# The first stage of a two-layer trunk on one Trainium2 core: modulation made tile by tile, x loaded first, and a third a_u head in the stage

## The chip, the cores and the metric

The kernel runs on one core of one Trainium2 chip. TensorE multiplies matrices, VectorE (DVE) and ScalarE (ACT) do elementwise work, GpSimd (POOL) some small arithmetic, and SyncE (SP) issues all transfers from memory. The time is the device time of one execution in microseconds, given as the median of several runs. The matrices are in float32, kept exact by splitting each operand into a rounded part and a rest, so that one product becomes three matmuls.

## The reference

Two layers act on a latent stream x (256 tokens, 2048 features) and a context stream of the same size. Each layer first scales and shifts the normalised stream, with a scale and a shift that come from a vector c:

```python
shift, scale, gate = jnp.split(silu_c @ w_mod[l] + b_mod[l], 3, axis=-1)
shift_c, scale_c, gate_c = jnp.split(silu_cc @ w_mod[l] + b_mod[l], 3, axis=-1)
h = rmsnorm(x, g_pre[l]) * (1.0 + scale[:, None]) + shift[:, None]
h_c = rmsnorm(ctx, g_pre[l]) * (1.0 + scale_c) + shift_c
proj = h @ w_in[l]
proj_c = h_c @ w_in[l]
```

The 5120 columns of the projection feed three branches: a gated MLP with position mixing (columns a_u, a_v, a_g), windowed attention (q, k, v, b_g) and a Fourier mixing (c_x, c_g). In the first branch y_a = gelu(a_u) * mix(rmsnorm(gelu(a_v))) * silu(a_g), with four heads of 128 columns. The branches are joined, multiplied by w_out, normalised, gated and added to the stream. The output is the latent stream after the second layer.

## The kernel before

Features are cut into 16 k tiles of 128. The two streams stand side by side, features on partitions, as 16 tiles of 128 x 512: `yo[k]` holds x, and `hh[k]`, `hl[k]` hold the two parts of h. A weight of `w_in` is streamed in halves of a unit (128 x 1024, 512 KB): SP loads it to `raw` (three buffers), ScalarE casts it to `whi` (L367), VectorE takes the rest as `wlo` (L368; four buffers each). `W.next` hands out the next half and emits those that are to be made ahead; `NEAR` says how many at the start of a layer. TensorE's order is exactly that of the program. The other engines' orders are made by a planner, which goes by priority (program order, unless lowered) and lets an instruction whose buffer is not free be passed by another.

The modulation vector needs w_mod, whose shift and scale columns of layer 0 are 33.6 MB. `mod_start` makes them on TensorE in the first stage: for a group of four k tiles of c (`kg` 0 to 3) it loads a block of w_mod and issues four products with c as the 128 x 32 stationary operand, one for each quadrant of the bank `ps_mod` (L172). VectorE transposes the bank (L177), four small products sum the quadrants into `ps_modc` (L182), and VectorE makes `gs` and `sh`, the scale and shift of the tiles (L191 to L194). k tiles 0 to 7 go in four pairs (`PAIRS`, products 512 wide, loads of 256 KB into the buffers of the still unused tiles hh8 to hh15 and hl8 to hl15), k tiles 8 to 15 one by one (`ALONE`, products 256 wide, 512 KB loads or two of 256 KB). For the single tiles there are two sets of buffers, for even and for odd k.

`make_h` (L451, L455, L458) then turns x into h, and the loop over `blocks` in `layer` accumulates, k outermost, four banks of a_v (tokens on partitions, 12 matmuls a tile) and two banks of a_u (heads 0 and 1, six matmuls a tile), while the next block's modulation runs between. These six banks have the tag `mm`; the remaining two banks of PSUM have the tag `ms` and serve ps_mod, ps_modc and all small results. After the stage `branch_a` and `fourier_mats` are queued as later work, which is given back to TensorE in the middle of the following units when a count of product time (`later.tick`) has reached its due time. Then come units of 128 columns (`tunit`, 48 matmuls into `ps_t`): the heads 2 and 3 of a_u, c_x and so on. The rest of w_mod is multiplied on VectorE in steps that `pace` issues at a rate per unit.

At the start SP issues c, the vectors, the first constants, then x. ScalarE squares x tile by tile (L464, L467), VectorE adds the squares (L468), TensorE sums them over features (L427, L429), GpSimd takes the power (L414), VectorE and TensorE spread the result (L421, L433) and VectorE copies it as `rb0` (L1009). In TensorE's order this lies between the first groups of the first modulation block.

Of the kernel before, what the change touches and what calls it, by code (L numbers as in the profile page):

```python
# [13 lines left out]
P = 128  # L14
# [9 lines left out]
PAIRS, ALONE = [0, 2, 4, 6], list(range(8, KT))  # L24
# [3 lines left out]
def units():  # L28
    """(name, first column, columns, first k tile, k tiles): blocks of w_in of 128 x 2048 each."""
    u = []  # L30
    u += [("av", COL["av"], 512, 4 * i, 4) for i in range(4)]
    u += [("au01", COL["au"], 256, 8 * i, 8) for i in range(2)]
    u += [(f"au{h}", COL["au"] + 128 * h, 128, 0, 16) for h in (2, 3)]
    u += [(f"cx{h}", COL["cx"] + 128 * h, 128, 0, 16) for h in range(4)]
    u += [(f"ag{h}", COL["ag"] + 128 * h, 128, 0, 16) for h in range(4)]
    u += [(f"cg{h}", COL["cg"] + 128 * h, 128, 0, 16) for h in range(4)]
    u += [(f"k{h}", COL["k"] + 128 * h, 128, 0, 16) for h in range(2)]
    u += [("v", COL["v"], 256, 8 * i, 8) for i in range(2)]
    u += [(f"q{h}", COL["q"] + 128 * h, 128, 0, 16) for h in range(8)]
    u += [(f"bg{h}", COL["bg"] + 128 * h, 128, 0, 16) for h in range(8)]  # L40
    return u
# [25 lines left out]
def trunk_kernel(ctx: ExitStack, tc: tile.TileContext, xT, xhalf, cT, wss, wsl, wmod, win, wout0, wout1, const, vec, rows,  # L67
# [24 lines left out]
    # ---- constants  # L92
    ct = sb([P, KT, 2], F32, "ct")
    DMA.dma_start(ct, cT)
    vecs = sb([P, 2, NVEC], F32, "vecs")
    DMA.dma_start(vecs, vec)
# [13 lines left out]
    class low:  # L110
        """instructions that may wait for the next `n`."""
# [22 lines left out]
    # ---- modulation: columns [128, 16, stream] of scale, shift and gate  # L134
# [5 lines left out]
    def mod_cols(l, cb, ps8):  # L140
        """ps8 [128, 4, 2]: silu(c) @ w_mod for 512 columns of column block cb."""
        what, j0 = cb // 4, (cb % 4) * 4
        b = vc(l, "bmod")[:, cb * 4:cb * 4 + 4].unsqueeze(2).to_broadcast([P, 4, 2])
        sl = slice(j0, j0 + 4)
        if what == 0:
            V.tensor_tensor(out=sh[l][:, sl], in0=ps8, in1=b, op=ALU.add)
        else:
            dst = (gs[l] if what == 1 else gg0)[:, sl]
            g = vc(l, "gpre" if what == 1 else "gpost")[:, sl].unsqueeze(2).to_broadcast([P, 4, 2])
            V.scalar_tensor_tensor(out=dst, in0=ps8, scalar=1.0 if what == 1 else 0.0, in1=b,  # L150
                                   op0=ALU.add, op1=ALU.add)
            V.tensor_tensor(out=dst, in0=dst, in1=g, op=ALU.mult)

    def mod_start(k0, nk):
        """scale and shift of k tiles k0 .. k0 + nk - 1 of layer 0 on the tensor engine: yields after
        each unit's products, and before the columns."""
        ps = ms_ps("mod")
        n = 2 * P * nk
        for kg in range(4):
            src = wss[PAIRS.index(k0), kg] if nk == 2 else wsl[ALONE.index(k0), kg]  # L160
            if nk == 1:
                tags = (("mraw", "mraw", "macc", "vv"), ("mg", "mgl", "yo0 yo1", "yo2 yo3"))[k0 % 2][kg]
            else:
                tags = " ".join(f"{t}{8 + 2 * kg + i}" for i in range(2) for t in ("hh", "hl"))
# [31 lines left out]
    def mod_dve(l, cb, red):  # L196
        """red [128, 2, 16]: sums over the 32 partitions of each quadrant, transposed."""
# [38 lines left out]
    def mod_gate1():  # L236
        """products of silu(c) and the gate's columns of w_mod in layer 1, still to be summed over partitions."""
# [16 lines left out]
    def gate1():  # L254
        """(sum + b_mod) * g_post of layer 1's gate, on all partitions."""
# [23 lines left out]
    NEAR = [1] * 6 + [0] * 6 + [1, 2, 3]  # L279
# [7 lines left out]
    def pace():  # L287
        """steps of the modulation due per half of a unit, behind the latest weights on the vector engine."""
# [6 lines left out]
    # ---- work of other engines that hands products back to the tensor engine later  # L295
    class Later:
# [19 lines left out]
        def flush(self):  # L316
# [8 lines left out]
            (("yo8 yo9", 1), ("yo10 yo11", 1)), (("yo12 yo13", 1), ("yo14 yo15", 1))]  # L325
    BACK = 8

    # ---- weights: raw -> exact parts hi + lo, in halves of a unit, ahead of their use
    class Stream:
        AHEAD = 3  # L330

        def __init__(self):
            self.src, self.out, self.pos, self.stop = [], [], 0, 0
            self.place, self.behind = {}, {}
            for l in range(2):
                def half(name, i, h):
                    return win[l, UIDX[name][i], h]
                for i in range(2):
                    self.src += [half("av", 2 * i, 0), half("au01", i, 0), half("av", 2 * i, 1),
                                 half("av", 2 * i + 1, 0), half("au01", i, 1), half("av", 2 * i + 1, 1)]  # L340
                for i, u in enumerate(UNITS):
                    if u[0] not in ("av", "au01"):
# [45 lines left out]
    def part(w, c):  # L388
        """columns c of both parts; a part is a tile or a list of tiles side by side."""
# [19 lines left out]
    # ---- per-token reciprocal rms from sums over features  # L409
# [14 lines left out]
    def col_sums(ps, q, n, start=True, stop=True):  # L424
        """columns of ps: sums over the partitions of q [128, n * 128], one accumulation group."""
# [10 lines left out]
    # ---- streams in feature-major tiles  # L436
    yo = [None] * KT
# [7 lines left out]
    def make_h(l, k, rb, streams):  # L445
        """h = x * rstd * gs + sh, as hi + lo; rb: rstd over the tokens of `streams`."""
# [26 lines left out]
    def tunit(n, sl=None):  # L473
        """feature-major product of one unit of 128 columns: PSUM [128, n]."""
# [18 lines left out]
    blocks = [(k, 2) for k in PAIRS] + [(k, 1) for k in ALONE]  # L493

    # ---- one layer, up to the inputs of the output projection
    def layer(l):
# [12 lines left out]
        # a_v (token-major) and two heads of a_u, k outermost  # L509
        av = [mm_ps("av") for _ in range(nt)]  # L510
        au = [mm_ps("au") for _ in range(2)]
# [6 lines left out]
        def start_au(k):  # L518
            for j in range(2):
                c = slice((k % 4) * 256 + j * P, (k % 4) * 256 + (j + 1) * P)  # L520
                mm3(au[j][:, 0:n], part(auw, c), (hh[k][:, 0:n], hl[k][:, 0:n]), k == 0, k == KT - 1)
            later.tick(PASS * 512 * nt + PASS * n * 2)

        for i, (k0, nk) in enumerate(blocks):
# [13 lines left out]
            if k0 % 4 == 0:  # L538
                auw = W.next()
            for _ in range(2 if nk == 2 else 4):  # L540
# [38 lines left out]
        # branch A  # L579
        def branch_a():  # L580
            vt = [w2k([P, 512]) for _ in range(nt)]
            ss = sb([P, 4], F32, "ss")
            for j in range(2):
# [8 lines left out]
            yield 12.0 if l == 0 else 7.0  # L592
            for h in range(4):
# [9 lines left out]
                yield (12.0 if h == 1 else 2.0) if l == 0 else (7.0 if h == 1 else 2.0)  # L603

        # branch C
# [9 lines left out]
        def fourier(g, ps):  # L615
            """cos(2 pi t m / 256) is even in t around 128 and sin odd: positions t and 256 - t are added for the one
            and subtracted for the other, which leaves 128 rows each (position 128 in the sines' row of t = 0)."""
# [25 lines left out]
        # branch B  # L643
        def rope(hi, lo, ps):
            """x * cos + rot(x) * sin of the latents, and x of the context, as hi + lo."""
# [97 lines left out]
        for h in (2, 3):  # L743
# [56 lines left out]
    # ---- output projection  # L800
# [33 lines left out]
    def finish():  # L834
        """layer 1's output projection with tokens on partitions, and x1 + gate * y / rms(y)."""
        x1 = {}

        def turn():
            """x1 of the latents to tokens on partitions: [128, token tile, 512] per 512 columns."""
# [68 lines left out]
    def boundary(s, acc):  # L908
        """x1 = x0 + gate * y / rms(y) of stream s in place, and its own 1 / rms."""
# [79 lines left out]
    with tc.manual_schedule(engines={mybir.EngineType.PE}):  # L989
        # ---- start: modulation of the first k tiles, x and its statistics  # L990
        raw = w2k([P, NFIRST])
        DMA.dma_start(raw, const[:, 0:NFIRST])
        A.copy(identr, raw[:, 0:P])
        A.copy(cst[:, 0:NFIRST - P], raw[:, P:])
        for k in range(KT):
            yo[k] = sb([P, T], F32, f"yo{k}")
            DMA.dma_start(yo[k], xT[k])
        acc0 = sb([P, T], F32, "acc")
        for k in range(KT):
            add_sq(acc0, yo[k], FULL, k == 0)  # L1000
        m = mod_start(*blocks[0])
# [9 lines left out]
        W.emit()  # L1011
        W.emit()
# [82 lines left out]
```

## Time and profile before

| | us |
|---|---|
| time, median of 3 runs | 1171.78 (1170.43 to 1172.42) |
| span of the profiled execution | 1167.9 |
| TensorE busy in it | 1136.0 (97%) |
| VectorE busy | 881.8 (76%) |
| ScalarE busy | 509.8 (44%) |
| first a_v product starts | 37.37 |
| first product of the unit after the stage | 136.79 |

The median of the runs lies 3.9 us above the span of the profiled execution; no time of its own is given for that execution. In the lines of the profile, `ps_t<-hh,whi` means that the tile ps_t is written from hh and whi, `x48` is a count, and L172 is line 172 of the kernel. The chain of work that ended last is followed back from the last instruction, so a piece on it is work, or a wait counted into the piece before it, that the end hangs on. A busy share of 97% on TensorE is not a measure of its speed: products are pipelined, and their ends are modelled.

### The profile page before, as it was taken

To read this page: it belongs to the slowest core of one execution; us is meant where nothing else is said; L and a number is where in the kernel's file an instruction comes from. 1 tells how busy PE (TensorE), PEld (TensorE's weight loads), DVE (VectorE), ACT (ScalarE), POOL (GpSimd) and SP (SyncE) were. 2 spreads that over 40 slices of the span, in tenths; PEclk is the share of its full clock that TensorE was granted. 3 is DMA by queue.
4 is the path that set the end of the run, shared out by engine and by line. 5 is a ranking of instruction groups with operands and counts; after the bars stand their busy time and mean duration, and the time that the engine had idled before them with its cause. 6 is when DMAs were issued, how large, how long until landed. Compare 5 with 4: busy or idle time off the path is not lost.

```text
span 1167.9 us, 17483 instructions
## 1 busy us (share of the span) xinstructions
PE 1136.0 (97%) x6656; PEld 953.7 (82%) x6656; DVE 881.8 (76%) x1469; ACT 509.8 (44%) x914; POOL 17.3 (1%) x23
## 2 busy tenths in 40 slices
PE   3999999999999999999999999999999999999996
PEld 1466688888898888888888888889899999997885
DVE  5454498888988878798989886495896678888554
ACT  4222513322224667632533233365563278745442
POOL 0000000000000000000000000200000000000001
PEclk9999999999999999999999999999999999999998
DMA  9999765466665334455466665365656665688563
GB/s 339 378 387 357 254 196 166 145 202 193 200 200 178 105 114 136 134 175 173 158 199 209 205 216 162 109 207 173 205 158 205 203 200 178 195 269 244 190 187 120
DMA packets 73892, 234.32 MB, mean 201 GB/s; under 512 B 8528, under 2 KB 9680, under 8 KB 73808
## 3 DMA queue, kind: packets, MB, share of 16 engines
q1 hardware_dynamic: 73808, 233.21, 61.6%
q8 instruction: 52, 0.85, 0.3%
q14 instruction: 32, 0.26, 0.1%
HBM read 231.08 MB, written 2.10 MB: 200 GB/s over the span
## 4 chain that ended last, share of the span: by engine, by line
PE 92%; DVE 3%; DMA 2%; ACT 2%; issue 1%; POOL 0%; SPq 0%; DVEq 0%; ACTq 0%; POOLq 0%
PE ps_t L384 20%; PE ps_t L385 20%; PE ps_t L386 20%; PE ps_mod L172 3%; PE ps_av L384 2%; PE ps_y L386 2%; PE ps_y L384 2%; PE ps_y L385 2%; PE ps_av L385 2%; PE ps_av L386 2%; PE ps_v L386 1%; PE ps_v L384 1%; PE ps_v L385 1%; PE ps_tp L722 1%; PE ps_au L384 1%
## 5 line engine op out<-in xcount | busy, mean ns | idle before, releaser
L384 PE MATMUL ps_t<-hh,whi 128*128 128x512 f32 (+1 forms) x1296 | 452.1, 349 | 0.0
L386 PE MATMUL ps_t<-hh,wlo 128*128 128x512 f32 (+1 forms) x1296 | 447.4, 345 | 0.0
L385 PE MATMUL ps_t<-hl,whi 128*128 128x512 f32 (+1 forms) x1296 | 447.0, 345 | 0.0
L367 ACT CAST whi<-raw 128x1024 fp32r<-128x1024 f32 x218 | 228.2, 1050 | 397.3 <-PE ps_t L385 274.4
L368 DVE TENSOR_TENSOR wlo<-raw,whi 128x1024 fp32r<-128x1024 f32 x218 | 265.3, 1220 | 99.1 <-ACT whi L367 98.8
L384 PEld LDWEIGHTS ps_t<-hh,whi 128*128 128x128 f32 x1296 | 244.9, 189 | 34.3 <-issue 4.6
L386 PEld LDWEIGHTS ps_t<-hh,wlo 128*128 128x128 f32 x1296 | 244.7, 189 | 30.6
L385 PEld LDWEIGHTS ps_t<-hl,whi 128*128 128x128 f32 x1296 | 244.9, 189 | 28.9 <-issue 0.5
L209 DVE SCALAR_TENSOR_TENSOR macc<-mraw,cs,macc 128x512 f32<-128x512 f32 x360 | 249.9, 745 | 17.6 <-DMA mraw<-in_wmod_dram 17.5
L455 ACT ACTIVATE hh<-w2k,sh 128x256 fp32r<-128x256 f32 x64 | 29.0, 502 | 61.4 <-DVE w2k L451 61.4
L384 PE MATMUL ps_y<-whi,hh 128*128 128x512 f32 x112 | 45.0, 401 | 0.0
L386 PE MATMUL ps_y<-whi,hl 128*128 128x512 f32 x112 | 43.8, 392 | 0.0
L385 PE MATMUL ps_y<-wlo,hh 128*128 128x512 f32 x112 | 43.7, 390 | 0.0
L384 PE MATMUL ps_av<-whi,hh 128*128 128x512 f32 x96 | 40.0, 416 | 0.0
L385 PE MATMUL ps_av<-wlo,hh 128*128 128x512 f32 x96 | 37.9, 395 | 0.4 <-DVE wlo L368 0.4
L172 PE MATMUL ps_mod<-hh,kt 128*32 128x512 f32 x64 | 21.5, 649 | 17.0 <-DMA hh<-in_wss_dram 17.0
L386 PE MATMUL ps_av<-whi,hl 128*128 128x512 f32 x96 | 37.6, 392 | 0.0
L386 PE MATMUL ps_v<-whi,hl 128*128 128x256 f32 x128 | 36.2, 283 | 0.0
L384 PE MATMUL ps_v<-whi,hh 128*128 128x256 f32 x128 | 36.2, 283 | 0.0
L385 PE MATMUL ps_v<-wlo,hh 128*128 128x256 f32 x128 | 36.2, 283 | 0.0
L468 DVE TENSOR_TENSOR acc<-acc,w2k 128x512 f32<-128x512 f32 (+1 forms) x33 | 21.2, 641 | 18.7 <-ACT w2k L467 17.2
L401 ACT CAST w2k<-ps_tp 128x512 fp32r<-128x512 f32 x40 | 23.5, 587 | 22.8 <-PE ps_scc L385 12.0
(292 smaller groups left out, 1491.8 us busy)
## 6 DMA issues: line engine op xcount, KB each, us to landing
raw<-in_win_dram SPq DMA_DIRECT2D x160, 512.0 KB, 4.1
mraw<-in_wmod_dram SPq DMA_DIRECT2D x128, 512.0 KB, 4.3
raw<-in_wout_dram SPq DMA_DIRECT2D x64, 512.0 KB, 4.2
hh<-in_wss_dram SPq DMA_DIRECT2D x32, 256.0 KB, 5.6
hl<-in_wss_dram SPq DMA_DIRECT2D x32, 256.0 KB, 5.4
yo<-in_xT_dram SPq DMA_DIRECT2D x16, 256.0 KB, 5.4
mraw<-in_wsl_dram SPq DMA_DIRECT2D x8, 512.0 KB, 6.9
yo<-in_wsl_dram SPq DMA_DIRECT2D x16, 256.0 KB, 7.2
```

Of the source, the lines that this page charges most:

```text
L172: PE.matmul(ps[32 * kk:32 * kk + 32, 0:n], cpad[:, kg * 4 + kk], ws[kk], start=kg == 0, stop=kg == 3, tile_position=(0, 32 * kk))
L209: V.scalar_tensor_tensor(out=acc[:, s], in0=w[:, kk % 2], scalar=c, in1=acc[:, s], op0=ALU.mult, op1=ALU.add)
L367: A.copy(ph, r[:, c])
L368: self.last = V.tensor_tensor(out=pl, in0=r[:, c], in1=ph.bitcast(F32), op=ALU.subtract)
L384: PE.matmul(ps, st[0], mv[0], start=start, stop=False)
L385: PE.matmul(ps, st[0], mv[1], start=False, stop=False)
L386: PE.matmul(ps, st[1], mv[0], start=False, stop=stop)
L401: A.copy(hi, src)
L455: first = A.activation(hh[k][:, sl], t[:, sl], AF.Identity, bias=sh[l][:, k, s:s + 1])
L468: V.tensor_tensor(out=acc[:, sl], in0=acc[:, sl], in1=q[:, sl], op=ALU.add)
L722: PE.transpose(tp[:, (2 * j + b) * P:(2 * j + b + 1) * P], src, ident)
```

## The change

Layer 0's first stage is rewritten in three respects. All sixteen k tiles get their modulation one by one (`blocks` holds single tiles only), with other buffers for the odd tiles below 8. x is loaded first, with c behind its first tile, and the first constants and the vectors behind x; ScalarE's two copies of the constants come after the squares. And a third head of a_u (head 2) is accumulated in the stage, in one of the two `ms` banks, with its two weight halves in the buffers named in `AU2`; the unit au2 behind the stage goes, three halves are emitted before the stage instead of two, and the due times of `branch_a` in layer 0 are 9.0 and 4.0 instead of 12.0 and 12.0. Layer 1 keeps its two heads in the stage.

```diff
-PAIRS, ALONE = [0, 2, 4, 6], list(range(8, KT))
+PAIRS, ALONE = [0], list(range(KT))
...
-    ct = sb([P, KT, 2], F32, "ct")
-    DMA.dma_start(ct, cT)
+    yo = [sb([P, T], F32, f"yo{k}") for k in range(KT)]
+    for k in range(KT):
+        DMA.dma_start(yo[k], xT[k])
+        if k == 0:
+            ct = sb([P, KT, 2], F32, "ct")
+            DMA.dma_start(ct, cT)
     vecs = sb([P, 2, NVEC], F32, "vecs")
-    DMA.dma_start(vecs, vec)
...
-                tags = (("mraw", "mraw", "macc", "vv"), ("mg", "mgl", "yo0 yo1", "yo2 yo3"))[k0 % 2][kg]
+                odd = ("hh14 hl14", "hh15 hl15") if k0 < 8 else ("yo0 yo1", "yo2 yo3")
+                tags = (("mraw", "mraw", "macc", "vv"), ("mg", "mgl") + odd)[k0 % 2][kg]
...
-    NEAR = [1] * 6 + [0] * 6 + [1, 2, 3]
+    NEAR = [1] * 7 + [0] * 7 + [1, 2, 3]
...
+    AU2 = [(("hh12 hl12", 1), ("hh13 hl13", 1)), (("yo4 yo5", 1), ("yo6 yo7", 1))]
...
-                    self.src += [half("av", 2 * i, 0), half("au01", i, 0), half("av", 2 * i, 1),
+                    third = [half("au2", 0, i)] if l == 0 else []
+                    if l == 0:
+                        self.place[len(self.src) + 2] = AU2[i]
+                    self.src += [half("av", 2 * i, 0), half("au01", i, 0), *third, half("av", 2 * i, 1),
                                  half("av", 2 * i + 1, 0), half("au01", i, 1), half("av", 2 * i + 1, 1)]
...
-                    if u[0] not in ("av", "au01"):
+                    if u[0] not in ("av", "au01") + ("au2",) * (l == 0):
...
-    blocks = [(k, 2) for k in PAIRS] + [(k, 1) for k in ALONE]
+    blocks = [(k, 1) for k in ALONE]
...
-        au = [mm_ps("au") for _ in range(2)]
+        au = [mm_ps("au") for _ in range(2)] + [ms_ps("au") for _ in range(1 - l)]
...
+            if l == 0:
+                mm3(au[2], part(au2w, slice((k % 8) * P, (k % 8 + 1) * P)), (hh[k], hl[k]), k == 0, k == KT - 1)
...
+            if k0 % 8 == 0 and l == 0:
+                au2w = W.next()
...
-            for j in range(2):
+            for j in range(len(au)):
                 A.activation(ytmp(j), au[j][:, 0:n], AF.Gelu_apprx_tanh)
...
-            yield 12.0 if l == 0 else 7.0
+            yield 9.0 if l == 0 else 7.0
...
-                yield (12.0 if h == 1 else 2.0) if l == 0 else (7.0 if h == 1 else 2.0)
+                yield (4.0 if h == 1 else 2.0) if l == 0 else (7.0 if h == 1 else 2.0)
...
-        for h in (2, 3):
+        for h in range(len(au), 4):
...
         raw = w2k([P, NFIRST])
         DMA.dma_start(raw, const[:, 0:NFIRST])
-        A.copy(identr, raw[:, 0:P])
-        A.copy(cst[:, 0:NFIRST - P], raw[:, P:])
-        for k in range(KT):
-            yo[k] = sb([P, T], F32, f"yo{k}")
-            DMA.dma_start(yo[k], xT[k])
+        DMA.dma_start(vecs, vec)
         acc0 = sb([P, T], F32, "acc")
         for k in range(KT):
             add_sq(acc0, yo[k], FULL, k == 0)
+        A.copy(identr, raw[:, 0:P])
+        A.copy(cst[:, 0:NFIRST - P], raw[:, P:])
...
-        W.emit()
-        W.emit()
+        for _ in range(3):
+            W.emit()
```

1 line of the change is left out of this document (removed).

## The prediction

> **What bounds the kernel now.** I read the page from its second part, because the change touches one stage only, and that part says where each engine works along the span.
>
> ```profile
> PE   3999999999999999999999999999999999999996
> DVE  5454498888988878798989886495896678888554
> DMA  9999765466665334455466665365656665688563
> GB/s 339 378 387 357 254 196 166 145 202 193 200 200 178 105 114 136 134 175 173 158 199 209 205 216 162 109 207 173 205 158 205 203 200 178 195 269 244 190 187 120
> ```
>
> One digit is 29.2 us. TensorE is idle for a good part of the first slice and then busy to the end; the transfers run at 340 to 390 GB/s in the first four slices, which is the stage that the change rewrites, and at half of that later. So what TensorE saves there should be saved in the end, unless the transfers of the stage hold it up. Next I read the chain that ended last, asked for the first 95 us (columns: start, length, what).
>
> ```profile
> 17.02 3.83 PE ps_mod L172 x8
> ...
> 24.50 2.04 PE ps_rb L433 x2
> 26.54 4.14 PE ps_mod L172 x16
> ...
> 31.82 5.56 PE ps_mod L172 x16
> 37.37 0.43 PE ps_av L384
> ...
> 41.70 2.83 PE ps_mod L172 x16
> ...
> 49.24 1.85 PE ps_mod L172 x16
> ...
> 62.06 2.27 PE ps_mod L172 x15
> ...
> 86.32 1.86 PE ps_mod L172 x32
> ...
> 91.18 0.17 PE ps_modc L182 x8
> ```
>
> The first a_v product starts at 37.3. Before it, ps_mod of the first pair and half of the second pair waits for its weights: 4.14 and 5.56 us for blocks that take 1.86 when the weights are there. After 37.3 the chain stays on TensorE; only two blocks exceed 1.85, at 41.70 by 0.98 and at 62.06 by 0.42. Last, the engines by stretch (busy us and count of TensorE, its weight loads, VectorE, ScalarE, GpSimd; granted clock; DMA share; GB/s).
>
> ```profile
> 17.00:20.80 3.80, 3.78 (x9) 0.74 (x9) 1.96 (x3) 0.00 (x0) 0.00 (x0) 1.00 1.04 384
> 24.50:26.40 1.90, 1.90 (x2) 0.47 (x2) 0.00 (x0) 0.79 (x1) 0.00 (x0) 0.50 1.00 392
> 26.40:28.00 1.60, 1.60 (x10) 0.33 (x10) 1.42 (x2) 1.30 (x2) 0.00 (x0) 0.56 1.05 388
> 33.00:37.30 4.30, 4.30 (x13) 0.76 (x12) 3.66 (x8) 1.49 (x4) 0.00 (x0) 1.00 1.05 387
> 86.30:93.00 6.70, 6.70 (x63) 4.40 (x66) 1.81 (x7) 0.67 (x2) 0.00 (x0) 1.00 0.85 272
> 99.50:106.00 6.50, 6.50 (x59) 4.28 (x58) 2.55 (x8) 0.88 (x3) 0.00 (x0) 1.00 1.01 395
> ```
>
> Until 37.3 the bytes set the time (385 to 392 GB/s). From 86.3 on, where k tiles already go one by one, TensorE does: a tile takes 6.58 us (a_v starts at 88.19 and 127.68, six tiles), and the loads wait for freed buffers.
>
> **The change, part by part.** The sum is made against the profiled execution, whose span is 1167.9; the median of 1171.78 lies 3.9 above that span, and I take those 3.9 as what lies around it.
>
> 1. *The first a_v starts earlier.* Before, 12.2 MB must land ahead of it: x (4.19), the small constants (0.19), pair 0 of the modulation (4.19), three weight halves (1.57), half of pair 1 (2.10). The last load arrives at 36.33, so at 0.388 MB/us the stream counts as begun at 4.8. After, it is x, constants, tile 0 (2.10), tile 1 (2.10), three halves, and perhaps the fourth half, which the third `W.next` now asks for ahead of tile 1's loads: 10.15 or 10.67 MB, 26.2 or 27.5 us. Putting x first saves three issues, 1.38 us (SP's 0.74 to 2.12); const and vec, now behind x, still pass ahead of the modulation with 0.17 MB, 0.45 us, so the stream begins 0.9 earlier, at 3.9. Tile 1 is complete at 30.1 or 31.4; its last products and the gap to a_v take 1.0 in the row before (36.33 to 37.30), of products twice as wide, so 0.5 to 1.0. First a_v: between 30.6 and 32.4. I take 31.7, near the later end, because SP took every half in this stage in program order. Gain 5.6 (4.9 to 6.7). The constants that now come behind x are not missed: identr is first needed at 23.48, ct for the products at 17.02, vecs at 31.87, and they land by some 16. ScalarE's two copies (0.30, 0.21) come after the squares, where it waits 8.71 us for weights. The sum of squares ends at 19.17 and its chain to rb0 at 27.27; tile 0's columns then need some 3 us to become h, by about 30.5, beside the loads of tile 1, so this hides.
>
> 2. *One modulation block more behind the first a_v.* Before, three tiles' worth of ps_mod lies ahead of it and 13 behind; after, two and 14. A block of 32 entries takes 1.86 and about 0.1 at each end: +2.07.
>
> 3. *Four more column steps* (L182: 15 behind the first a_v instead of 11), each 0.35 to 0.37 between a_v and a_u (91.11 to 91.28 and the wider first a_u spacing): +1.5. Their VectorE operations (L191 to L194, 0.16 each) have room: VectorE idles 1.1 to 2.7 us before each in the single-tile part.
>
> 4. *The two waits of 0.98 and 0.42 go*: -1.4 (0 if they come back elsewhere). A tile now costs TensorE 6.58 + 3 x 0.231 = 7.28 us. It brings 2.10 MB plus 0.46 of weights (0.066 more than before), 6.6 us at 388 GB/s, so 0.7 us a tile are left and the loads should run ahead.
>
> 5. *The third head.* 48 products at 0.231 (the spacing of both ps_au and ps_t) come into the stage, 11.1, and the unit au2 of 48 at the same spacing goes: 0. The 1 MB of weights only moves. The wait before the first unit (0.4 behind Gelu L584 by the waits of ps_t, 0.25 on the chain) goes behind the third head's last three products, as do bits of the start-up of each phase: -0.6, or 0.
>
> 6. *One slot of the two `ms` banks is held by the third head.* ps_mod and ps_modc share the other. The column step needs the transpose anyway; the new wait is ps_mod of the next tile for VectorE to read ps_modc. The reads end 0.35 us after the column step, up to 1.2 more behind one split (L368); nine a_u products (2.08 us) lie between. 0; if VectorE were later still, each us would queue a_v, a_u and everything behind it.
>
> 7. *After the stage.* the mod steps of `pace` come two later: its rates sum to 104.8 steps in layer 0 instead of 106.8, and 96 are needed; two splits and their work leave VectorE together with the unit. branch_a's first mix is now due 9 units in, which is 9.7 us of products and 1.72 of ps_mg after the stage. Its inputs were ready at 146.98, 10.2 after the stage's end, and the third Gelu adds 0.60: 10.8 against 11.4. Cover 0.6; I take +0.3 (0 to +2).
>
> Sum: -5.6 + 2.07 + 1.5 - 1.4 - 0.6 + 0.3 = -3.7. Checked by construction: 31.7 + 14 x 7.28 + 5.41 + 4.83 (the last two tiles, 4.72 and 4.39 before, plus 0.69, less the Gelu wait) = 143.9, where the remaining unit begins; before, au3 would begin at 136.8 + 11.1 = 147.9. That is -4.0, with the mix -3.7. So span 1164.2, time 1168.1.
>
> [...] The row first: after TensorE had waited 1.37 us for VectorE at 23.13, the granted clock was 0.50 from 24.5 to 26.4 and 0.56 to 28.0, and products took 1060 ns that take 592 at full clock. The chain after shows TensorE again waiting for loads just before its first a_v. In this trace the like stretch (33.0 to 37.3) kept clock 1.00, so the sum has no such cost. [...]
>
> **The rivals.** *A. SP stands behind the fourth weight half.* Its buffer is one of three `raw` and comes free only when the first half has been split; before, that split ended at 28.4, behind the rb0 copy (26.58). If SP issues in program order it stands there until about 27.4, with the six loads of tile 1 behind it; these then land from 3.9 us later (x's first load took that) at 1.35 us per 512 KB: first a_v at 37.4, no gain of item 1. The rest of the sum is +1.8: 1173.6. It decides against the change when the first a_v comes after 35.5. For it: every half of this stage was issued where the program has it, and SP waited on wlo L368 for 8.7 us up to 136. Against: the planner let loads with free buffers pass one without (skb at 121.13 ahead of the w2k load at 135.78), and tile 1's buffers are free from the start; and the first half now lands about 5 us earlier.
>
> *B. The first a_v runs at half clock.* One stretch as at 24.5 to 28.0, 3.3 us at half speed, costs 1.65: 1169.8. For it, the row above; against it, 33.0 to 37.3.
>
> *C. The mix comes due too early.* ScalarE's order after the stage (casts of 1.05 among the Gelus) puts the inputs later by two casts, 2 us, and TensorE, in program order, waits: 1169.8. For it: only 0.6 of cover; against: three units' time had been given before.
>
> *D. The transfers bound the stage.* If the rate falls to the 355 GB/s of the windows around 93 and 119, a tile takes 7.2 us, still under 7.28: no cost. Below 352 GB/s (2.56 MB in 7.28 us) each 10 GB/s cost 0.2 us a tile; at 330 it is 7.76, +0.5 on 14 tiles, 7 us: 1175. Against it: those windows are low because buffers were full.
>
> **How the numbers follow.** The forecast has 0.62 (1166 to 1169.8 by itself: the start of a_v by -1.1 and +0.7, items 4 and 5 by up to +2, the mix by up to +1.7). A 0.12, B 0.10, C 0.10, D 0.04, others 0.02. About 0.2% (2.3 us) is what can be told from no change, so faster means under 1169.4. Of the forecast's 0.62 some 0.53 lie there, and 0.04 each of B and C: 0.61. A and D are 1173.6 and more; 1174.1 is the limit for slower, but the mechanism of A and a misjudged order of the engines after the stage could add: 0.08 of A, 0.04 of D and 0.01 of the rest make 0.13. The remainder, 0.26, is the same. The range goes from 1165.6 to 1172.6, leaving out most of A and D and a small lower tail; the likeliest is 1168.1.
>
> **What would show it.** The first ps_av at 30.6 to 32.4; a_v starts 7.28 apart from then on, with 1.86 us for each mod block; the remaining tunit beginning near 144 and the first ps_t of cx0 about 4 us earlier than before; the same shift at every later mark. It is wrong if SP shows a gap before the loads of tile 1 (A), if TensorE's clock in the stretch of the first a_v is below 1 (B), if ps_mix waits for w2k L591 (C), if ps_mod waits for in_wsl after tile 3 (D), or if ps_mod waits for VectorE's sh L194 (item 6).

## The result, and the profile after

The changed kernel takes 1179.85 us (median of 5 runs, 1174.52 to 1182.35) against 1171.33 (5 runs, 1170.43 to 1172.42): ratio 1.0072, 95% interval 1.0049 to 1.0094. It is slower, by 0.7%; the forecast was 1168.1, a gain. Each run's time lies 1.8 above the span of the same execution; the span profiled here, 1172.7, belongs to the quickest of the five, and the one of before (1167.9, so some 1169.7) to the quick end of its own. So the two traces, 4.8 apart, show a little more than half of the 8.5 between the medians. The prediction had taken 3.9 as what lies around the span; 1.8 of that does, and the other 2.1 is that the profiled execution of before was a quick one.

The page after, second part:

```profile
PE   1999999999999999999999999999999999998996
DVE  5444578889887787798989996586796678987554
DMA  9999664555664343355466665365655665677563
GB/s 331 392 345 341 246 206 160 175 180 194 215 198 162 115 147 108 119 178 181 140 226 201 232 203 164 110 209 176 198 162 202 206 201 178 199 267 237 180 193 115
```

TensorE does less in the first slice than before (1 instead of 3), and the rate of the first four slices is no higher (352 GB/s in the mean, 365 before). The start is read from the chain of the changed kernel (start, length, what):

```profile
14.20 6.98 DMA raw<-in_win_dram
21.20 1.05 ACT whi L375
...
23.42 0.70 DVE acc L475
24.16 1.88 PE ps_rs L437 x8
26.30 1.42 POOL rs_b L422
...
28.77 2.05 PE ps_rb L441 x2
30.82 1.70 PE ps_mod L176 x16
...
33.38 1.83 PE ps_mod L176 x32
35.20 0.43 PE ps_av L392
```

What bounds the start is no longer the modulation's bytes. The chain goes through a load of *weights* (raw), its cast, and then the last add of squares, which stands behind a weight split on VectorE. VectorE's own rows say it outright; first those of before, then those of the changed kernel:

```profile
11.31 7.86 DVE L468 TENSOR_TENSOR acc<-acc,w2k 128x512 f32<-128x512 f32 x10
...
27.19 2.35 DVE L368 TENSOR_TENSOR wlo<-raw,whi 128x1024 fp32r<-128x1024 f32 x2
```

```profile
11.87 5.47 DVE L475 TENSOR_TENSOR acc<-acc,w2k 128x512 f32<-128x512 f32 x7
22.27 1.23 DVE L376 TENSOR_TENSOR wlo<-raw,whi 128x1024 fp32r<-128x1024 f32 x1 [4.94 <-ACT whi L375]
23.42 0.68 DVE L475 TENSOR_TENSOR acc<-acc,w2k 128x512 f32<-128x512 f32 x1
```

Before, all adds end at 19.17 and the splits come 8 us later. Now there are seven adds, then 4.94 us of waiting for ScalarE's cast, the split, and only then the last add, on which the whole row from ps_rs to rb0 hangs. SP's rows show the gap that the prediction's rival A described. SP issues the fourth weight half when the first split frees its buffer, and the loads of tile 1 (from mg on) behind it; the last of them is issued at 26.44 and lands 6.5 us later, at 32.97:

```profile
15.96 0.48 SPq L173 DMA_DIRECT2D vv<-in_wsl_dram  x1
23.53 0.33 SPq L366 DMA_DIRECT2D raw<-in_win_dram  x1
23.90 0.43 SPq L173 DMA_DIRECT2D mg<-in_wsl_dram  x1
```

Within the stage the chain is as forecast; a_v starts 7.24 to 7.27 apart in every tile but the last, and a modulation block takes 1.86:

```profile
85.95 0.43 PE ps_av L392
...
91.33 1.86 PE ps_mod L176 x32
93.20 0.43 PE ps_av L392
```

Three more places differ. ScalarE at the stage's end:

```profile
141.71 1.98 ACT L375 CAST whi<-raw 128x1024 fp32r<-128x1024 f32 x2
145.03 1.05 ACT L375 CAST whi<-raw 128x1024 fp32r<-128x1024 f32 x1 [1.33 <-issue]
146.10 1.28 ACT L596 ACT_TABLE_LOAD   x1
147.39 1.58 ACT L596 ACTIVATE yo<-ps_au 128x512 f32<-128x512 f32 x3
```

Three casts precede the Gelu (two before), and the unit after the stage starts at 148.04, 1.04 us of idle TensorE after the stage's last product. Then, far behind the stage, the chain from 695 to 719:

```profile
702.19 1.51 DVE macc L213 x3
...
706.08 5.16 DMA raw<-in_wout_dram
...
711.34 1.06 ACT whi L375
...
714.32 1.22 DVE mraw L219 x2
...
716.02 0.66 DVE red L220
...
717.79 1.23 DVE mraw L376
...
719.06 0.39 PE ps_t L394
```

These are the last steps of the modulation's second part (macc, the transpose into mraw, the sum red); a weight half that is to be held in the buffer mraw (`place`, `HELD`) comes after them, and ps_t waits for it, on TensorE 1.74 us:

```profile
719.06 0.39 PE L394 MATMUL ps_t<-hh,mraw 128*128 128x256 f32 x1 [1.74 <-DVE mraw L376]
```

Before, VectorE had this order too, but finished the sum at 710.8 instead of 716.7, and no product waited:

```profile
710.11 0.69 DVE L216 TENSOR_REDUCE red<-mraw 128x16 f32<-128x512 f32 x1
710.88 1.22 DVE L368 TENSOR_TENSOR mraw<-raw,mraw 128x1024 fp32r<-128x1024 f32 x1
```

Last, layer 1's first stage, where VectorE's rows after

```profile
757.87 0.48 DVE L458 SCALAR_TENSOR_TENSOR w2k<-yo,gs,rbs 128x256 f32<-128x256 f32 x1
758.99 0.48 DVE L465 SCALAR_TENSOR_TENSOR hl<-w2k,sh,hh 128x256 fp32r<-128x256 f32 x1 [0.64 <-ACT hh L462]
759.92 3.50 DVE L376 TENSOR_TENSOR wlo<-raw,whi 128x1024 fp32r<-128x1024 f32 x3 [0.45 <-ACT whi L375]
```

differ from those of before, in which two tiles of h come first:

```profile
756.44 0.88 DVE L451 SCALAR_TENSOR_TENSOR w2k<-yo,gs,rbs 128x256 f32<-128x256 f32 x2
757.57 0.89 DVE L458 SCALAR_TENSOR_TENSOR hl<-w2k,sh,hh 128x256 fp32r<-128x256 f32 x2 [0.24 <-ACT hh L455]
758.91 2.36 DVE L368 TENSOR_TENSOR wlo<-raw,whi 128x1024 fp32r<-128x1024 f32 x2 [0.46 <-ACT whi L367]
```

With three splits ahead of the second tile's h, ps_av waits for it:

```profile
PE ps_av L392 <- ACT hh L462: 1.4, 1, 1.4
```

Layer 1's loop goes over the same list `blocks` that the change cut to single tiles.

### The profile page after: what moved, and what is told of

Read it like the earlier page. It is cut to its first block, busy times and chain, and to the rows that moved or that the text cites. A ratio compares the mean times of both kernels' runs of the same rounds, so it can differ in the third digit from the quotient of the medians.

```text
span 1172.7 us, 17778 instructions
## 1 busy us (share of the span) xinstructions
PE 1128.7 (96%) x6816; PEld 958.6 (82%) x6816; DVE 883.8 (75%) x1487; ACT 510.2 (44%) x917; POOL 17.9 (2%) x23
## 4 chain that ended last, share of the span: by engine, by line
PE 71%; DVE 13%; DMA 9%; ACT 3%; issue 3%; POOL 0%; SPq 0%; DVEq 0%; ACTq 0%; POOLq 0%
PE ps_t L392 14%; PE ps_t L394 13%; PE ps_t L393 13%; DMA mraw<-in_wmod_dram 6%; DVE macc L213 4%; DVE wlo L376 3%; PE ps_mod L176 3%; PE ps_av L392 2%; PE ps_y L392 2%; PE ps_y L394 2%; PE ps_y L393 2%; PE ps_av L393 2%; PE ps_av L394 2%; PE ps_au L392 1%; PE ps_v L394 1%
## 5 line engine op out<-in xcount | busy, mean ns | idle before, releaser
L392 PE MATMUL ps_t<-hh,whi 128*128 128x512 f32 (+1 forms) x1280 | 445.7, 348 | 1.0 <-ACT yo L596 1.0
L394 PE MATMUL ps_t<-hh,wlo 128*128 128x512 f32 (+1 forms) x1280 | 440.7, 344 | 0.0
L393 PE MATMUL ps_t<-hl,whi 128*128 128x512 f32 (+1 forms) x1280 | 440.6, 344 | 0.0
L376 DVE TENSOR_TENSOR wlo<-raw,whi 128x1024 fp32r<-128x1024 f32 x216 | 262.6, 1219 | 107.3 <-ACT whi L375 106.8
L392 PEld LDWEIGHTS ps_t<-hh,whi 128*128 128x128 f32 x1280 | 242.2, 189 | 34.4 <-issue 4.6
L394 PEld LDWEIGHTS ps_t<-hh,wlo 128*128 128x128 f32 x1280 | 242.2, 189 | 29.1
L393 PEld LDWEIGHTS ps_t<-hl,whi 128*128 128x128 f32 x1280 | 242.3, 189 | 27.6 <-issue 0.5
L409 ACT CAST w2k<-ps_tp 128x512 fp32r<-128x512 f32 x40 | 23.4, 586 | 22.5 <-PE ps_scc L393 12.0
L465 DVE SCALAR_TENSOR_TENSOR hl<-w2k,sh,hh 128x256 fp32r<-128x256 f32 x64 | 28.3, 480 | 3.0 <-ACT hh L462 3.0
L662 ACT COPY mgl<-ps_t 32x256 f32<-32x256 f32 x80 | 29.1, 364 | 1.2 <-PE ps_t L394 0.2
```

The lines of the kernel that those rows point to most:

```text
L376: self.last = V.tensor_tensor(out=pl, in0=r[:, c], in1=ph.bitcast(F32), op=ALU.subtract)
L392: PE.matmul(ps, st[0], mv[0], start=start, stop=False)
L393: PE.matmul(ps, st[0], mv[1], start=False, stop=False)
L394: PE.matmul(ps, st[1], mv[0], start=False, stop=stop)
L409: A.copy(hi, src)
L465: last = V.scalar_tensor_tensor(out=hl[k][:, sl], in0=t[:, sl], scalar=sh[l][:, k, s:s + 1], in1=hh[k][:, sl].bitcast(F32), op0=ALU.add, o ...
```

## The experiments

All times below are medians with their range; each ratio is against the kernel before, run beside it on the same chip. The table gives, for each profile, when the first a_v product itself starts (37.30 before; the chain's row stands at 37.37), and by how much six later products start later than in the profile of before (these marks stand there at 184.87 ps_z, 511.30 ps_o, 736.62 ps_rs, 797.28 ps_mg, 1062.22 ps_y and 1095.27 ps_x). Each row is one execution. The two profiles of before differ by 0.6 to 0.7 at the first a_v and at every mark up to 1062, so a single difference of that size between two rows shows nothing.

| profile | first a_v | 185 | 511 | 737 | 797 | 1062 | 1095 |
|---|---|---|---|---|---|---|---|
| before | 37.30 | 0 | 0 | 0 | 0 | 0 | 0 |
| before, again | 37.9 | -0.63 | -0.66 | -0.66 | -0.64 | -0.73 | -0.17 |
| changed | 35.13 | +0.23 | +0.24 | +1.39 | +2.87 | +2.95 | +5.07 |
| steps earlier, in cx0 | 36.84 | +2.11 | +1.50 | +0.66 | +2.13 | +2.32 | +4.44 |
| start order, first form | 33.7 | -1.21 | -1.16 | +3.52 | +4.99 | +5.63 | +8.57 |
| Gelu first | 35.55 | +0.25 | +0.73 | +7.81 | +9.29 | +9.49 | +13.58 |
| these three | 33.43 | -0.81 | +1.53 | +0.69 | +2.14 | +2.28 | +4.50 |
| pairs in layer 1 | 34.8 | -0.14 | -0.06 | +1.35 | +1.39 | +1.52 | +2.27 |
| steps earlier, in q0 | 35.83 | +0.91 | +1.03 | +0.19 | +1.67 | +1.90 | +4.17 |
| four repairs | 31.69 | -3.90 | -3.55 | -4.39 | -4.08 | -3.27 | -1.77 |
| singles alone | 32.27 | -3.34 | -3.93 | -4.77 | -3.32 | -3.09 | -1.66 |
| x first alone | 38.11 | +0.97 | +0.96 | +0.96 | +0.97 | +0.92 | +1.71 |
| x first and singles | 34.62 | -1.00 | -1.61 | -2.45 | -0.97 | -0.83 | +1.29 |
| start repair alone | 31.13 | -3.22 | -3.17 | +1.05 | +2.51 | +2.59 | +2.89 |
| singles, pairs in layer 1 | 32.83 | -2.82 | -3.44 | -4.28 | -4.25 | -4.15 | -2.55 |
| singles, steps late | 32.30 | -2.45 | -2.42 | +0.28 | +1.77 | +1.83 | +3.24 |

My theory after the two traces was that three losses had taken the gain: the order of VectorE and SP at the start, the Gelu at the stage's end, and the two steps that come later. The rival was that the third head or the single tiles cost in themselves.

**Steps earlier, in cx0.** The changed kernel with a higher rate of steps in a phase before the late ones.

```diff
-    RATE = dict(au0=2, cx0=2.2, ...
+    RATE = dict(au0=2, cx0=2.7, ...
```

> The changed kernel with the rate of w_mod steps in the phase cx0 raised from 2.2 to 2.7, so that the two steps lost with the unit au2 are made up there. Theory 'late steps': the steps end as early as before, the wait of ps_t behind the split into mraw (1.9 us near 726) goes, the boundary's first column sums come 0.2 us instead of 1.4 us later than in the kernel before, and the time falls by 1.2 to 2.7 us against the changed kernel. Rival 'only the start and the stage': the two late steps hide nothing and delay nothing, the time stays where the changed kernel has it (1174.5 to 1182.4) and the spread of its runs stays too.

1173.89 (1171.31 to 1177.06), ratio 1.002 (1.0007 to 1.0034). The loss between 511 and 737 is gone, and with it 0.5% of the time: 6.0 us at the medians, where 1.2 to 2.7 had been expected from the one quick profile.

**Start order, first form.** The first three weight halves are handed out behind the rb0 copy, and the fourth is asked for later.

```diff
-    NEAR = [1] * 7 + [0] * 7 + [1, 2, 3]
+    NEAR = [1, 1, 0, 1, 1, 1, 1] + [0] * 7 + [1, 2, 3]
...
-        for _ in range(3):
-            W.emit()
+        with tc.issue_after(spread.ins):
+            for _ in range(3):
+                W.emit()
```

> The changed kernel with the splits of the first three weight halves ordered behind the copy rb0, and the fourth half not asked for until k tile 2. Theory 'order at the start': the last add of squares follows its square at about 17.5 instead of 23.4, SP does not stand at the fourth half, the first a_v starts at 30 to 32 instead of 35.2, and all later marks of layer 0 move by the same 3 to 5 us. Rival 'bytes': the loads of k tile 1 land as late as the chain of squares allowed anyway, the first a_v stays at 34 to 35, the time within 1 us of the changed kernel.

1177.71 (1173.53 to 1179.63), ratio 1.0047 (1.0026 to 1.0067). The first a_v comes at 33.7, not at 30 to 32: TensorE stood from 27.0 to 30.0, and the modulation block behind that took 3.35, at a granted clock of 0.54 from 30.0 to 33.7. The late wait stayed, at 3.3 and 0.9.

**Gelu first.** The last of the three casts that stood ahead of the first Gelu (that of the 17th weight half) is put behind it.

```diff
-                A.activation(ytmp(j), au[j][:, 0:n], AF.Gelu_apprx_tanh)
+                first = A.activation(ytmp(j), au[j][:, 0:n], AF.Gelu_apprx_tanh)
+                if l == 0 and j == 0:
+                    W.behind[16] = (first,)
```

> The changed kernel with the cast of the 17th weight half ordered behind the Gelu of the first a_u head at the end of the stage. Theory 'cast ahead of the Gelu': ScalarE loads its table before 145 and the unit au3 starts at 146.9 instead of 148.0, a gain of 1.1 us that stays to the end of layer 0. Rival: the cast is then late for the second half of the unit and TensorE waits there instead, gain 0.

1179.91 (1175.14 to 1183.01), ratio 1.0072 (1.0045 to 1.0099): no gain. The wait of ps_t for the Gelu is gone, but with the first a_v 0.4 later the mark at 185 is where it was. The wait for the Gelu is real; by these two profiles it is worth about 0.4 and not the 1.1 expected, and 0.4 is within what two profiles of one kernel differ by.

**These three together.**

> The changed kernel with all three edits: steps, start order, Gelu. Theory 'three orders': the gains add up, 1.2 + 4 + 1.1, and the time is 1166 to 1169, under the kernel before. Rival 'something later': the mean of the changed kernel, 1179.85, lies 5 us above its profiled execution, so part of the loss has a cause that none of the edits touches; then the time stays above 1171.

1173.14 (1170.70 to 1174.85), ratio 1.0012 (1.0003 to 1.0021): above 1171, as the rival had it. What the start gained is lost by 213 us (+1.02 there): in the units that cx0's additional steps fall on, ps_f and ps_z wait 3.0 us for copies to w2k, 2.5 of them VectorE's (L410) and 0.5 ScalarE's (L409). That the steps alone do this is not shown: steps earlier in cx0, with the same rate and a later start, has none of these waits. The steps were then tried in another phase.

**Before, again.** The question was whether the profile of before is a lucky one.

> The kernel before, unchanged, for a second profiled execution. The first had a span of 1167.9, and each run since lies 1.5 to 1.8 above its span, so it stands for a time of about 1169.6, faster than the median of 1171.3 to 1171.8. Theory 'lucky profile': the second has a span of 1168 to 1170, and what it loses against the first lies behind 1060 us, where TensorE waits for the gate's products (ps_x behind ctrh). Rival: the spans agree within 0.3 us, and the 3.9 us are work outside the span.

One run, 1169.49, span 1167.7: the spans agree within 0.2, but time and span are again 1.8 apart and not 3.9, and the run is again at the quick end of those of before (1168.86 to 1172.55 beside it). Its finish varies by itself (+0.56 from 1062 to 1095).

**Pairs in layer 1.** The changed kernel, whose layer 1 goes over the old pairs.

```diff
+    pairs = [(k, 2) for k in range(0, 8, 2)] + [(k, 1) for k in range(8, KT)]
...
-        for i, (k0, nk) in enumerate(blocks):
+        for i, (k0, nk) in enumerate(pairs if last else blocks):
```

> The changed kernel, but layer 1 goes through its first stage in the blocks of the kernel before (four pairs, then single tiles). Theory 'shared list': the list blocks serves both layers, and with single tiles layer 1 asks for its weights after one h instead of two, so that three splits stand ahead of the second tile's h at 760; undone, the 1.45 us that every changed kernel loses between 755 and 797 come back, and nothing else changes: 1.5 us less than the changed kernel. Rival 'planner': the order there comes from the earlier shift in time, and the 1.45 us stay.

1175.89 (1171.70 to 1181.09), ratio 1.0045 (1.0027 to 1.0062). The 1.48 between 737 and 797 is gone (+1.35 to +1.39). The median is 4.0 lower than that of the changed kernel, but the runs are spread as widely, so how much of the 4.0 is layer 1 can't be read from it.

**Steps earlier, in q0.** One number of the changed kernel: q0=2.05 in place of 1.8 in `RATE`.

> The changed kernel with the two lost steps made up in the phase q0 (rate 2.05 instead of 1.8), where VectorE is busy for 31 to 34 of 40 us, and not in cx0, where it was full. Theory 'late steps': the waits of ps_t behind the splits into mraw go as with the rate in cx0, the boundary's mark at 736 is 0 to 1 us behind layer 0's other marks, and the time falls to 1172 to 1175, with the spread of the kernel before. Rival 'cx0 only': in q0 the steps delay the attention's work, and the time stays above 1176.

1172.89 (1171.41 to 1174.63), ratio 1.0013 (1.0004 to 1.0022). Seven of the 8.5 us between the medians, and the spread, go with two steps that come earlier.

**Four repairs.** q0=2.05, Gelu first, pairs in layer 1, and a start order in which the first split comes behind the diagonals (L429), the second behind the rb0 copy, the third behind tile 0's columns, and the fourth half is asked for later (`NEAR`).

> The changed kernel with all repairs: the first split behind the diagonal, the second behind rb0, the third half asked for after tile 0's columns, the fourth not until tile 2; the Gelu ahead of the cast; the steps made up in q0; pairs in layer 1. Theory 'four orders': the first a_v at 30.5 to 32, layer 0's marks 3 to 5 us ahead of the kernel before and kept to the end, 1166 to 1169. Rival 'taken back later': VectorE, full behind the stage, loses what the stage gains; marks at 500 us less than 1 us ahead, time 1170 to 1172.

1168.13 (1166.34 to 1169.69), ratio 0.9974 (0.9962 to 0.9986). The first a_v comes at 31.69, and the kernel is faster than before.

**The parts one by one.** Then the change was taken apart: single tiles alone (`PAIRS`, `blocks` and the buffers of odd tiles), x first alone (the loads' order and the two copies), and both without the third head.

> The kernel before with single k tiles alone: load order and two heads in the stage as before. Theory of the parts: two single modulation blocks stand ahead of the first a_v in place of one pair and half of another, 2.1 MB less to load, so the first a_v comes at about 33.5 (before 37.3); one mod block more (2.07), four column steps (1.5) and two waits fewer (1.4) leave the marks at 185 to 736 us about 1.5 below before, with no waits of ps_t for mraw between 511 and 736; layer 1, which shares the list of blocks, gives 1.45 back by 797. Net about 0: 1171.5. Rival (singles cause the loss of the start): first a_v at 36 or later, marks at +1 and more, and 1173.5 or more.

1167.83 (1165.92 to 1170.41), ratio 0.9973 (0.9962 to 0.9984): this part alone is as good as the whole change with four repairs. The expectation of 1171.5 and of a first a_v at 33.5 was too late: it comes at 32.27, and a tile of two heads every 6.58.

> The kernel before with x loaded first and the constants behind it, pairs and two heads as before. Theory of the parts: the loads begin 0.9 earlier, so the first a_v comes about 0.9 earlier (36.4), no split of weights stands ahead of the last add of squares, and all later marks are 0.9 below before: 1170.8, within noise of before. Rival (x first alone causes the loss of the start): the last add of squares waits for a split, the chain to rb0 ends after 28, first a_v at 37.3 or later, marks at 0 or above.

1171.29 (1169.56 to 1175.49), ratio 0.9998 (0.9988 to 1.0008). The expected 36.4 did not come: the first a_v is at 38.11, against 37.30 and 37.91 in the two profiles of before. SP issues the last load of x 0.9 earlier, but the first load of the modulation, behind the constants, at 11.95 instead of 11.46.

> The changed kernel without its third head: single k tiles and x first, two heads in the stage, due times of branch_a as before. Theory of the parts: the loss of the start needs these two together (the first weight half lands while squares are still being added), so the first a_v comes at about 35 as in the changed kernel, marks at 185 to 511 about 0 to -1; the steps of the late w_mod columns come where they came before, so no ps_t waits for mraw between 511 and 736 (mark at 736 equal to that at 511 within 0.3), and the changed kernel's spread of 8 us shrinks to that of before (some 2 to 4); layer 1 gives 1.45 back. Time about 1172. Rival (the third head is not what makes the steps late): the mark at 736 rises by over 1, and runs go up to 1178 and more.

1170.80 (1169.78 to 1173.71), ratio 0.9998 (0.9989 to 1.0008). The split stands ahead of the last add here too (VectorE idle 4.63 before it), and the first a_v comes at 34.62. But SP does not stand:

```profile
15.62 0.45 SPq L361 DMA_DIRECT2D raw<-in_win_dram  x1
16.12 0.43 SPq L172 DMA_DIRECT2D mg<-in_wsl_dram  x1
```

Without SP's gap of 7.1 us, the first a_v is only 0.5 earlier than in the changed kernel, although the last load of tile 1 lands at 29.95 instead of 32.97. So here the split ahead of the add sets the first a_v, and in the changed kernel it covers the gap. Singles alone and x first alone have all adds done by 18.8, so it takes both parts to put the split there. Nor is there a wait for mraw.

**Start repair alone.** The changed kernel with the start order of the four repairs (the splits and the later fourth half) and nothing else.

> The changed kernel with the start order of the best version alone: first split behind the diagonals, second behind the rb0 copy, third behind tile 0's columns, and the fourth half asked for later. Theory of the parts: the first a_v comes at 31.7 as predicted (changed kernel 35.1), marks at 185 to 511 are 3.4 below those of the changed kernel (about -3.2 against before); the waits of ps_t for mraw between 511 and 736 stay (+1 in a quick run, +7 in a slow one), as do 1.45 in layer 1: 1170 to 1178, a spread of 5 us or more. Rival (the start's gain is given back by TensorE's half rate or by Gelu at the stage's end): first a_v at 31.7 and marks at 185 of -1 or above.

1172.79 (1169.32 to 1176.03), ratio 1.0006 (0.9993 to 1.0020). The first a_v comes at 31.13, and the marks are 3.4 below those of the changed kernel up to 511; then 4.2 us are lost by 737. The waits of TensorE's weight loads between 511 and 757, and TensorE by stretch behind the wait (length, busy time and count of TensorE, weight loads, VectorE, ScalarE, GpSimd; granted clock, DMA share, GB/s):

```profile
PEld ps_t L394 <- DVE mraw L376: 3.3, 1, 3.3
```

```profile
717.00:719.00 2.00, 1.78 (x12) 1.78 (x13) 1.90 (x3) 0.00 (x0) 0.00 (x0) 0.83 0.70 262
719.00:721.00 2.00, 2.00 (x11) 2.00 (x11) 0.19 (x1) 1.05 (x1) 0.00 (x0) 0.50 0.98 334
```

In the changed kernel the wait was shorter and the clock stayed:

```profile
PEld ps_t L394 <- DVE mraw L376: 1.9, 1, 1.9
```

```profile
719.00:721.00 2.00, 1.94 (x16) 1.94 (x17) 1.74 (x3) 0.00 (x0) 0.00 (x0) 1.00 0.73 268
```

There are eleven products in two us instead of sixteen: the wait is paid once as idle time and again at half clock.

**Two open questions.** Whether late steps alone, without the third head, give this wait; and whether the gain from pairs in layer 1 lasts to the end.

> Single k tiles in layer 0 alone, as in the run before it, with layer 1 on its old list of pairs. Theory (the shared list costs layer 1 the 1.45 us between the marks at 736 and 797, seen so far only beside the late steps): the mark at 797 stays where that at 736 is (-4.8 against -4.8), the wait of the first tile's products for hh goes, and the time falls by about 1.4 to 1166.4. Rival (what layer 1 gains is lost again at the end, where the products ps_x wait for the gate's rows): marks 1.4 lower up to 1062 us, the same time as without it, 1167.8.

1166.24 (1164.26 to 1167.11), ratio 0.9954 (0.9937 to 0.9972), the quickest of all. The mark stays from 737 to 797 (-4.28 to -4.25), as the theory had it. Against singles alone 1.1 is left of the gain at 1062 and 0.9 at 1095. The time is 1.6 lower, but the two intervals overlap, so the second question is not settled by the times.

```diff
-    RATE = dict(au0=2, ...
+    RATE = dict(au0=1, ...
```

> Single k tiles alone, and the rate of the phase au0 halved (two units at 1 instead of 2), so that two steps of the late w_mod columns come later, as in the changed kernel, while the unit au2 stays where it was. Theory (the two steps are what costs, not the third head's buffers or bank): marks as with single tiles alone up to 511 us (-3.9); between 511 and 736 ps_t waits 1.9 us or more for mraw, and where the wait reaches some 3 us the granted clock halves for some us behind it, so the mark at 736 is 2 to 8 us higher than with single tiles alone (-4.8), the time 1170 to 1175 and the spread of the runs wider. Rival (the third head itself causes it): no such wait, 1167.8.

1172.04 (1168.16 to 1173.75), ratio 1.0006 (0.9995 to 1.0016). With two heads in the stage and only the steps late, the wait is there, in the waits of the weight loads, on TensorE and in the clock behind it:

```profile
PEld ps_t L387 <- DVE mraw L369: 2.0, 1, 2.0
```

```profile
716.43 0.39 PE L387 MATMUL ps_t<-hh,mraw 128*128 128x256 f32 x1 [1.77 <-DVE mraw L369]
```

```profile
717.00:719.00 2.00, 2.00 (x11) 2.00 (x11) 1.12 (x1) 0.00 (x0) 0.00 (x0) 0.50 0.88 299
```

The mark at 737 is 5.05 above that of singles alone (1.51 of it came by 511, which the expectation did not have), and the time 4.2. The late steps, not the third head's bank or buffers, are what costs.

## Why the prediction was wrong, point by point

The sum was -3.7 against the profiled execution; measured were +4.8 in the profiles and +8.5 at the medians. Of its terms, those for the stage itself held and those for what surrounds it did not. Two steps failed: that the sum of squares and its chain hide (item 1; 3.4 us at the first a_v), and that two later steps cost nothing (item 7; 2.0 in the profile, 7.0 at the medians with one number set back). Layer 1 (1.48) was left out.

*Item 1, the first a_v: mechanism right, price undone by an order.* 31.7 was forecast, 35.13 measured. The working counted bytes and let VectorE's work at the start hide. The bytes held: tile 1 was to be complete at 30.1 or 31.4, and its last load lands at 29.95 in start repair alone and at 30.56 in the four repairs. Its sentence that the sum of squares and its chain to rb0 hide beside tile 1's loads is the step that failed: the first weight split, whose load is now issued at 14.20 instead of 19.59, stands ahead of the last add, and ps_rb begins at 28.77 instead of the 22.81 of start repair alone. With that order mended the value is 31.13 and 31.69. The gain was the single tiles', 2.1 MB less ahead of the first a_v: alone they give 32.27. The 0.9 for an earlier stream did not come: x first alone has its first a_v 0.2 and 0.8 later than the two profiles of before.

*Rival A* was seen, but it does not set the changed kernel's first a_v: SP did stand at the fourth half from 16.4 to 23.5, yet x first with singles has no such gap and starts 0.5 earlier only. It is covered and not refuted. The gap moves tile 1's last load from 29.95 to 32.97, and every run that mends the order of the add also asks for the fourth half later, so what the gap would cost by itself is not shown.

*Items 2 to 4 held.* A tile takes 7.25 to 7.27 against 7.28; no wait on the transfers (*rival D*), 1.86 for each block. Singles alone check the sum: 32.27 is 5.03 earlier, plus 2.07 and 1.5, less 1.4, gives -2.9; the mark at 185 is -3.34. For the changed kernel, 2.17 earlier plus the same 2.17 gives 0; the mark is +0.23.

*Item 5* took 0 or -0.6. By the waits of ps_t the Gelu wait became 1.5 instead of 0.4 because a third cast preceded it; with that cast behind the Gelu it is gone. It counts for little: moving the cast left the mark at 185 unchanged, with a first a_v 0.4 later. *Item 6* held: ps_mod waits for no column step. *Rival C* did not come: ps_mix waits for nothing in the changed kernel.

*Item 7 is the main error.* It says that two steps come later, and puts that at 0 because the rates still give enough steps. That is not the question: the steps hold mraw and macc, and a weight half that goes into mraw must wait for the last of them. Before, VectorE had finished the last sum at 710.8 and that half at 712.1; after, at 716.7 and 719.0, with its product due at 717. In the kernels with single tiles and without the wait, the mark falls by 0.84 from 511 to 737 (why was not found). Against that the changed kernel's profile loses 2.0 there, start repair alone 5.1 and Gelu first 7.9. So the loss differs from profile to profile, as the times do. At the medians, the one number in q0 takes back 7.0. That is not a share of the 8.5: start repair alone takes back 7.1, though its marks up to 511 are only 3.4 lower, and pairs in layer 1 4.0, 18.0 together, where all four repairs give 11.7. These runs do not show why; a late wait whose size hangs on what comes before it would do so.

*Left out altogether* was layer 1, which uses the same list: it costs 1.48 from 737 to 797, which the three runs with pairs there cut to 0.03 to 0.31.

*Rival B* came, though not in the changed kernel's profiled execution: the second block took 1.83 there, and 3.33 to 3.52 in seven other kernels, 1.5 to 1.7 more. At the first a_v it can cost less: in start repair alone tile 1's last load lands at 29.95 and the first a_v starts 1.2 later.

What stays open: from 1062 to 1095 the changed kernel loses another 2.1 where ps_x waits for the rows of the gate (ctrh and nstrh), and the others between 0.3 and 4.1; the kernel before loses 0.56 there in its second profile against its first. What decides its size was not found. And the changed kernel's slowest executions were not traced themselves; that their time is the late wait rests on the kernels with the same steps whose profiles fell late in their range, and on the run with q0.

## What to carry to other kernels

When a unit of work is moved, count what rode on it: steps issued at a rate per unit come later with it, and what they cost is read at the first user of the buffers they hold, hundreds of microseconds on, and not from whether the steps suffice in number. When data arrive earlier, look at what an order by priority may now put ahead of the chain that sets the start. And before a list is changed for one stage, look for its other readers.

## What the runs showed of the hardware

In these runs a short wait of TensorE sometimes costs twice. Idle for 1.74 us at 717, the changed kernel went on at clock 1.00; idle for 1.77 at 714.7, singles with late steps ran at half clock for some 3.4 us (0.97, 0.50 and 0.68 in the three stretches of two us from 715 on; its products start 0.21 us apart from 716.89 to 720.30 and 0.12 behind that). In Gelu first, after waits of 1.82 and 3.11, the half clock lasts by the same column twice as long (0.71, 0.50, 0.50 and 0.59 from 721 on). So two waits 0.03 us apart in length had different clocks behind them; what decides it the rows do not show.

The column of the granted clock does not show all of it. In the changed kernel with steps earlier in cx0 the block behind the first columns took, by the chain,

```profile
33.42 3.49 PE ps_mod L176 x32
```

and with pairs in layer 1, with the same instructions before it,

```profile
33.04 1.83 PE ps_mod L176 x32
```

while the clock of the first reads 1.00 in every stretch from 24 to 38 us, as it does from 33.3 to 35.2 in the changed kernel, whose block took 1.83. The half rate is not new in that block: eight products of the first block, the same in form, take 1.08 us in both kernels (from 25.73 in the first, from 25.53 in the second), and in the changed kernel one of them takes 631 ns in the mean up to 27 us and 379 ns from 33.70 on. In the second kernel eight take 0.64 from 32.93 on; in the first they still take 1.08 and 1.11 from 33.27 on, and two of them 0.64 to 0.67 up to 36.27, against 0.39 to 0.41 in the second. Why it ends later in the one isn't shown.
